# A tuned single-core decoder layer: one block product of the input projection made by seven sub-products, for two pairs of column tiles at once

## The chip, the cores and the metric

The kernel runs on one core of one Trainium2 chip. The metric is the device time of one execution in microseconds (us); the time before is the median of three runs. The engines are named as in the profile: PE (matmul, with PEld for its weight loads), DVE, ACT, POOL, and SP, which here only issues DMAs.

## The reference, cut to what matters

One layer works on 1024 prompt tokens and 8 samples of 8 tokens. Everything starts from one wide projection; the rest (pooling branch, state-space branch, gated merge, output product, final norm) is not touched by the change.

```python
def layer(x, c, pos0, pool_buf, conv_buf, ssm_state, w_ada, b_ada, norm_g, w_in, ...):
    ...
    h = rmsnorm(x, norm_g) * (1 + scale[:, None]) + shift[:, None]
    proj = h @ w_in
    u_pool, z_pool, z_ssm, xbc, dt_raw, g_raw = jnp.split(proj, SPLITS, axis=-1)
    ...
    xbc_c, conv_new = causal_conv(xbc, conv_buf, conv_w, conv_b)
    ...
    x = x + gate[:, None] * (m @ w_o)
```

`h` has 1088 rows (tokens, prompt and samples together) and 1024 columns; `w_in` has 1024 rows and some 8000 columns. Everything is fp32.

## The kernel before, in words

**Numbers in two parts.** PE multiplies fp32r operands. To keep fp32 accuracy each operand is split into a high part (ACT copies it with rounding into a tile `whi`) and a low part (raw minus high, into `wlo`), and each product is three matmuls: high by high, high by low, low by high. `split` (L141) does this for a weight tile: one ACT instruction on L145, one subtraction on L148. In the stages of this case that subtraction is on POOL, the default of its argument `eng`. The parts of `h` stay in SBUF for the whole projection, in `hh_` and `hl_`.

**The projection in pairs.** `w_in` is worked through in pairs of column tiles of 128 columns. For a pair, the product of `h` (two halves of tokens by two halves of the inner dimension: A11, A12, A21, A22) with the weights (two halves of the inner dimension by two column tiles: B11, B12, B21, B22) is made by seven block products instead of eight, in `strassen` (L412). The sums of token blocks (`S1`, `S2`, `S3`, S4 in place of A21) are made once, ahead. The sums of weight blocks (t3 = B22-B12, t2 = t3+B11, t4 = t2-B21, d12 = B12-B11) are made for each pair in `steps` of `pair_w` on L347: three differences of 128x512 on DVE, one on POOL. One block product is one call of `product` (L402): two PSUM banks of 272 tokens, each with 12 matmuls (4 inner tiles by 3 terms), so 24 matmuls; seven of them are 168 matmuls for a pair. Each bank is read when its twelve are done: by ACT on L432 (the first product), by DVE on L419 (sums of partial results `s1`, `u2`, `u3`) or L424 (results of the pair). A12 B21 is one of the seven, and it enters only one of the four results.

**Stages.** 30 pairs go through `product`. The first 20 (the stage between 91 and 520 us, here called the weave) are `heavy` ones, which convolve on DVE (L1088, three instructions of 128x1112 for each column tile) or pool, mixed with `light` ones, which only pass a gate function on ACT and go to DRAM. The last 10 are light ones (`LAST = 10`, 520 to 767 us); between their products the samples' state-space work is put in. In the weave a scheduler sets the order on each engine by priorities and a timeline of its own; in most of the last ten PE's order is that in which the code is written (`in_line`). A pair's weights are prepared while the pair before runs: `between` takes a step of `prep_q` after some products. Beside the weave, `splits` prepares the weights of the two later output products (POOL on L285), one step after each product, paced by `n * 17 // 5`.

**Buffers.** PSUM has eight banks, of tags `mm` (3), `ps` (4) and `pc` (1); in the weave `product` takes them in turn by `banks_`, in the last ten from `ps` and `mm`. There are four `whi` and four `wlo` tiles, three `raw` tiles (sums of weight blocks) and three `rawA` (a column tile as loaded, 512 KB, issued by SP).

Of the kernel before, what the change touches and what calls it, by code (L numbers as in the profile page):

```python
# [8 lines left out]
F32 = mybir.dt.float32  # L9
# [5 lines left out]
PRI = 0  # L15
# [5 lines left out]
P = 128  # L21
# [25 lines left out]
def tile_pool_ssd_step(  # L47
# [89 lines left out]
    scT = const([P, KT, 32], "scT")  # L137
# [4 lines left out]
    def split(raw, kept=None, ncols=P, eng=None):  # L142
        hi = wp.tile([P, 4, P], F32R, tag="whi", name=nm("whi"), bufs=4)
        lo = wp.tile([P, 4, P], F32R, tag="wlo", name=nm("wlo"), bufs=4)
        ins = act(hi[:, :, :ncols], raw[:, :, :ncols], AF.Copy)  # L145
        if kept is not None:
            kept.append(ins.ins)
        (eng or nc.gpsimd).tensor_tensor(lo[:, :, :ncols], raw[:, :, :ncols], hi[:, :, :ncols].bitcast(F32), ALU.subtract)  # L148
# [29 lines left out]
    md = const([P, 16, 9], "md")  # L178
# [82 lines left out]
    def splits():  # L261
# [68 lines left out]
    def pair_w(c0, c1, pri, second, apart=False):  # L330
        def run():
            with tc.high_priority(pri):
                cols = []
# [5 lines left out]
            w = []  # L339

            def add(x):
                with tc.high_priority(pri):
                    w.append(split(x, highs))
# [5 lines left out]
            def steps():  # L349
                t3, t2 = raw_(), raw_()  # L350
                diff(t3, b22, b12)
                yield
                diff(t2, t3, b11, ALU.add)
                if second:

                    t4 = raw_()
                    add(b21)
                    add(t2)
                    add(t3)
                    diff(t4, t2, b21, eng=nc.gpsimd)  # L360
                    yield
                    diff(b12, b12, b11)
                    add(b12)
                    add(t4)
                    add(b22)
                    yield
                    return
                add(t2)
                add(t3)
                yield  # L370
                diff(b12, b12, b11)
                add(b12)
                add(b21)
                diff(t2, t2, b21, eng=nc.gpsimd)
                add(t2)
                add(b22)
                yield
            def apart_():
                t3, t2 = raw_(), raw_()
                fine["n1"] = lambda: add(b21)  # L380
                fine["nt3"] = lambda: diff(t3, b22, b12)
                fine["nt2"] = lambda: diff(t2, t3, b11, ALU.add)
                fine["n2"] = lambda: add(t2)
                fine["nd"] = lambda: diff(b12, b12, b11)

                def rest():
                    t4 = raw_()
                    add(t3)
                    diff(t4, t2, b21, eng=nc.gpsimd)
                    add(b12)  # L390
                    add(t4)
                    add(b22)
# [1896 lines left out]
```

## Time and profile before

| what | value |
|---|---|
| median of 3 runs | 1221.16 us (1219.87 to 1222.5) |
| span of the profiled execution | 1219.3 us |
| PE busy, share of the span | 1203.2 us, 99% |
| PEld busy | 1127.1 us, 92% |
| DVE busy | 937.9 us, 77% |
| POOL busy | 758.1 us, 62% |
| ACT busy | 654.7 us, 54% |
| granted TensorE clock, mean | 0.998 |

The profile gives the profiled execution by its span, from the first to the last instruction: 1219.3 us. The run's own time holds what lies around the span too; against the three times shown that is 0.6 to 3.2 us. Busy shares are means over stages with different limits, so the stages are read apart in what follows. A record of a DVE, ACT or POOL instruction begins when the engine takes it up, and so includes time in which it stands at a port.

### The profile page before, as it was taken

What the parts mean: (1) busy time and instruction counts of PE and PEld (TensorE: products, weight loads), DVE (VectorE), ACT (ScalarE), POOL (GpSimd) and SP (SyncE); (2) the same over time, 40 slices, a digit from 0 to 9 for tenths busy, and PEclk for the clock granted to TensorE, in tenths of its full rate; (3) what the DMA queues carried; (4) which work ended last, traced back from release to release, by engine and by line L of the source; (5) the groups of instructions that cost most, each with busy time, mean ns of one, the idle gap of its engine ahead of it and who ended that gap; (6) DMA issues with size and microseconds to landing.
All of it is one profiled execution on the core that took longest, in us unless ns stands there. A gap on an engine that the chain in (4) does not pass through costs nothing.

```text
span 1219.3 us, 25493 instructions
## 1 busy us (share of the span) xinstructions
PE 1203.2 (99%) x9330; PEld 1127.1 (92%) x9330; DVE 937.9 (77%) x1587; ACT 654.7 (54%) x1491; POOL 758.1 (62%) x677
## 2 busy tenths in 40 slices
PE   9999999999999999999999999999999999999997
PEld 8879999999999999999989899989888898999885
DVE  6993788877989578876676664686877889679976
ACT  6854366565656656454544344566676656312435
POOL 1137868875978778664676766155677758422661
PEclk9999999999999999999999999999999999999999
DMA  9835455564565545443656566898779888585794
GB/s 347 307 136 212 134 155 179 157 232 151 165 188 181 171 149 187 137 143 122 205 187 210 172 198 215 317 314 265 264 257 293 270 279 279 186 313 174 233 213 150
DMA packets 169845, 257.48 MB, mean 211 GB/s; under 512 B 32048, under 2 KB 88120, under 8 KB 169720
## 3 DMA queue, kind: packets, MB, share of 16 engines
q1 hardware_dynamic: 89256, 163.38, 40.3%
q10 hardware_dynamic: 78160, 88.27, 21.4%
q0 software_dynamic: 2304, 4.20, 2.0%
q8 instruction: 74, 1.21, 0.4%
q14 instruction: 51, 0.42, 0.1%
HBM read 170.69 MB, written 85.10 MB: 210 GB/s over the span
## 4 chain that ended last, share of the span: by engine, by line
PE 84%; DVE 6%; DMA 5%; ACT 3%; issue 1%; POOL 1%; SPq 0%; ACTq 0%; DVEq 0%
PE mm L410 23%; PE ps L410 23%; PE mm L221 14%; PE pc L410 5%; PE ps L1256 2%; PE pc L1542 2%; PE ps L2042 2%; PE ps L2040 2%; PE ps L2041 2%; PE ps L1259 2%; DMA wo<-ph 1%; DMA Y<-in_x_prompt 1%; DMA v<-ys 1%; DMA dec<-acs_d 1%; PE ps L1517 1%
## 5 line engine op out<-in xcount | busy, mean ns | idle before, releaser
L148 POOL TENSOR_TENSOR wlo<-rawA,whi 128x512 fp32r<-128x512 f32 x120 | 173.7, 1452 | 81.4 <-ACT whi L145 77.4
L221 PE MATMUL mm<-Y,whi 128*128 128x352 f32 (+1 forms) x960 | 195.7, 334 | 0.8 <-DVE G L1975 0.6
L148 POOL TENSOR_TENSOR wlo<-raw,whi 128x512 fp32r<-128x512 f32 x90 | 149.1, 1665 | 61.4 <-ACT whi L145 51.3
L221 PEld LDWEIGHTS mm<-Y,whi 128*128 128x128 f32 x960 | 159.1, 188 | 7.6 <-issue 4.6
L1088 DVE SCALAR_TENSOR_TENSOR GA<-GA,cvT,GA 128x1112 f32<-128x1112 f32 x72 | 133.8, 1863 | 0.1
L410 PE MATMUL mm<-Y,whi 128*128 128x272 f32 x800 | 119.0, 291 | 0.1
L410 PE MATMUL ps<-Y,whi 128*128 128x272 f32 x800 | 117.4, 289 | 0.0
L145 ACT ACTIVATE whi<-rawA 128x512 fp32r<-128x512 f32 x120 | 75.1, 627 | 76.1 <-PE ps L410 37.7
L145 ACT ACTIVATE whi<-raw 128x512 fp32r<-128x512 f32 x90 | 56.0, 629 | 98.9 <-DVE raw L347 35.2
L410 PEld LDWEIGHTS mm<-Y,whi 128*128 128x128 f32 x800 | 106.8, 188 | 1.8 <-DVE h L1360 0.3
L410 PEld LDWEIGHTS ps<-Y,whi 128*128 128x128 f32 x800 | 106.9, 188 | 0.8 <-issue 0.7
L221 PE MATMUL mm<-Y,wlo 128*128 128x352 f32 (+1 forms) x480 | 98.5, 327 | 0.0
L1244 ACT ACTIVATE dec<-dec,acT 128x128 f32<-128x128 f32 x256 | 78.8, 389 | 29.2 <-POOL dec L1240 29.2
L221 PEld LDWEIGHTS mm<-Y,wlo 128*128 128x128 f32 x480 | 81.7, 188 | 0.0
L1474 POOL TENSOR_TENSOR Y<-xb,Y 128x512 fp32r<-128x512 f32 x32 | 41.2, 1287 | 54.4 <-ACT Y L1472 54.4
L285 POOL TENSOR_TENSOR pw<-pw,ph 128x512 fp32r<-128x512 f32 x40 | 65.8, 1644 | 14.1 <-ACT ph L283 8.2
L410 PE MATMUL mm<-G,whi 128*128 128x272 f32 x480 | 71.4, 290 | 0.0
L410 PE MATMUL ps<-G,whi 128*128 128x272 f32 x480 | 70.4, 289 | 0.0
L410 PE MATMUL ps<-Y,wlo 128*128 128x272 f32 x400 | 66.6, 288 | 0.0
L410 PE MATMUL mm<-Y,wlo 128*128 128x272 f32 x400 | 66.6, 288 | 0.0
L410 PEld LDWEIGHTS mm<-G,whi 128*128 128x128 f32 x480 | 64.0, 188 | 0.9 <-issue 0.4
L410 PEld LDWEIGHTS ps<-G,whi 128*128 128x128 f32 x480 | 64.2, 188 | 0.4 <-issue 0.3
(582 smaller groups left out, 3172.9 us busy)
## 6 DMA issues: line engine op xcount, KB each, us to landing
rawA<-in_w_in SPq DMA_DIRECT2D x62, 512.0 KB
dec<-acs_d SPq DMA_DIRECT2D x32, 512.0 KB
xbc<-GA ACTq DMA_DIRECT2D x24, 512.0 KB
Y<-wo SPq DMA_DIRECT2D x10, 1024.0 KB
pw<-in_w_ssm_out ACTq DMA_DIRECT2D x32, 256.0 KB
ws<-ph ACTq DMA_DIRECT2D x32, 256.0 KB
ws<-pw ACTq DMA_DIRECT2D x32, 256.0 KB
h<-in_state_ssm SPq DMA_DIRECT2D x32, 256.0 KB
```

What stands on the lines that cost most here:

```text
L145: ins = act(hi[:, :, :ncols], raw[:, :, :ncols], AF.Copy)
L148: (eng or nc.gpsimd).tensor_tensor(lo[:, :, :ncols], raw[:, :, :ncols], hi[:, :, :ncols].bitcast(F32), ALU.subtract)
L221: mm(ps[:, :n], w[k // 4][h][:, k % 4, :], r[k][:, o:o + n], start=(j == 0), stop=(j == len(terms) - 1))
L285: nc.gpsimd.tensor_tensor(raw.bitcast(F32R), raw, hi.bitcast(F32), ALU.subtract)
L410: mm(p, w[j // 8][:, k], A(k, s)[j // 4 == 1], start=(j == 0), stop=(j == 11))
L1088: V.scalar_tensor_tensor(d[:, :n], rp[:, k:k + n], cvT[:, 24 * k + mc:24 * k + mc + 1], d[:, :n], ALU.mult, ALU.add)
L1244: act(dec[:, h], dec[:, h], AF.Exp, bias=acT[:, c, 8 * g + h:8 * g + h + 1], scale=-1.0)
L1256: mm(o[hh], xd[:S, 2 * q + hh, :], dec[:S, 2 * q + hh], start=True, stop=state is None)
L1259: mm(o[hh], state[:, h * 64:h * 64 + 64], cE[:, h], start=False, stop=True)
L1474: nc.gpsimd.tensor_tensor(yl[g][:, :, o:o + S], v, yhc.bitcast(F32), ALU.subtract)
L1542: mm(pu, bt, xw.rearrange("p h d -> p (h d)"), start=True, stop=True)
L2040: mm(ps, hi, y[:, k, c0:c0 + cw], start=(first and k == 0), stop=False)
```

## The change

The block product A12 B21 is no longer made for each pair alone. For two pairs in a row (kind "a" and kind "b") the two left column tiles are taken together: A12 (544 tokens by 512) times B21 of both tiles (512 by 256) is again split in 2 by 2 and made by seven sub-products of 272 tokens, 256 inner rows and 128 columns, in a new function `burst`. A sub-product is six matmuls of the same shape as before (2 inner tiles by 3 terms), so the two pairs take 42 matmuls for it where they took 48. 28 of the 30 pairs become 14 such pairs of pairs: nine in the weave, five in the last ten. The sums of A12's blocks (`js1`, `js2`, `js3`, and one that takes the place of A12's own corner) are made once by `joint_operands`, beside the first weave units. The weight sums of the burst are made for each pair of pairs in `joint_steps`, with the subtractions of the low parts on DVE (`eng=V`); the rows of `w_in` that it needs are loaded a second time. A kind-"a" pair begins the preparation of its own six weights in its burst.

Two sums are left in PSUM. In the burst, and in a pair of kind None, A12 B21 is added onto the bank that holds A11 B11, once ACT has read that; and in the weave ("chained") the last product is added onto the banks of the fifth, once DVE has read these, so that DVE's two additions for it go. The rest: two constants move to a pool that is closed earlier, the descriptor scratch of the DMAs that POOL issues goes from 16 KB to 2 KB (these three make room), the pace of `splits` is 19/5, the last ten have 80 steps where they had 70.

```diff
-    scT = const([P, KT, 32], "scT")
+    scT = tfp.tile([P, KT, 32], F32, tag="scT", name="scT", bufs=1)
...
-                at.setdefault(n * 17 // 5 + step, []).append((f, n))
+                at.setdefault(n * 19 // 5 + step, []).append((f, n))
...
+                if meta["kind"] == "a":
+                    for c in (c0, meta["mate"]):
+                        r = raw_()
+                        load(r, tiles_of(c)[:, 4:8])
+                        joint.append(r)
...
+                if meta["kind"] is None:
+                    add("b21", b21)
...
+            def part(x, *names):
+                with tc.high_priority(pri):
+                    hi, lo = split(x, highs, n=2 * len(names), eng=V)
...
+            def joint_steps():
+                wa, wb = joint
+                tt = raw_()
+                diff(tt[:, 2:4], wb[:, 2:4], wb[:, 0:2])
+                diff(tt[:, 0:2], tt[:, 2:4], wa[:, 0:2], ALU.add)
+                yield
+                part(wa, "b11", "b21")
+                diff(wb[:, 0:2], wb[:, 0:2], wa[:, 0:2])
+                part(tt, "t2", "t3")
+                diff(wa[:, 2:4], tt[:, 0:2], wa[:, 2:4])
+                yield
+                part(wb, "d12", "b22")
+                part(wa[:, 2:4], "t4")
+                yield
...
+    def burst(w, ra, rb):
+        def sub(n, x, use, on=None):
+            p = bank_() if on is None else on
...
+            for j in range(6):
+                k = j % 2
+                mm(p, w[n][j // 4][:, k], A(k)[j // 2 == 1], start=(j == 0 and on is None), stop=(j == 5),
+                   skip_group_check=on is not None)
...
+        b1 = sub("b11", "a11", keep)
+        sub("t2", "s2", add(rb[:, 0], ra[:, 0]))
+        yield
+        sub("b21", "a12", keep, on=b1)
+        sub("t3", "s3", add(ra[:, 1], rb[:, 0]))
+        yield
+        b4 = sub("d12", "s1", add(rb[:, 1], ra[:, 1]))
+        sub("t4", "a22", add(ra[:, 1], ra[:, 1], ALU.subtract))
+        yield
+        sub("b22", "s4", add(rb[:, 0], rb[:, 0]), on=b4)
...
+        def fifth(s, p):
+            out(d1, HF, u3, s1)(s, p)
+            if not chained:
+                add(u2, u2)(s, p)
...
+        product(w["b22"], s4_part, out(d1, 0, u2, u2), on=p5 if chained else None)
...
+            if kind == "a":
+                own = steps()
+                next(own)
+                ra, rb = tmp("c2"), tmp("rb")
+                r_next.append(rb)
+                for n, _ in enumerate(burst(jw, ra, rb)):
+                    between("j")
+                    if n == 1:
+                        next(own)
+                    yield
+                next(own)
...
-        if due[0] == 7 * LAST - 4:
+        if due[0] == 8 * LAST - 4:
...
-    nc = _bacc.Bacc("TRN2", target_bir_lowering=False, num_devices=1)
+    nc = _bacc.Bacc("TRN2", target_bir_lowering=False, num_devices=1, dynamic_dma_scratch_size=2048)
```

How the order moves is shown at two places in the weave; `xN` is a row of N equal instructions, and the numbers in the names are those of buffers. First PE, before: the first half of an A12 B21 of one pair (`G` tiles are parts of A12, `whi_558` and `wlo_559` the weights B21, `ps_592` the bank).

```order
L410 MATMUL ps_592_3799<-G_98_760,whi_558_3634 128x272
L410 MATMUL ps_592_3799<-G_100_765,whi_558_3634 128x272
L410 MATMUL ps_592_3799<-G_109_860,whi_558_3634 128x272
L410 MATMUL ps_592_3799<-G_105_846,whi_558_3634 128x272
L410 MATMUL ps_592_3799<-G_99_761,whi_558_3634 128x272
L410 MATMUL ps_592_3799<-G_101_766,whi_558_3634 128x272
L410 MATMUL ps_592_3799<-G_110_861,whi_558_3634 128x272
L410 MATMUL ps_592_3799<-G_106_847,whi_558_3634 128x272
L410 MATMUL ps_592_3799<-G_98_760,wlo_559_3635 128x272
L410 MATMUL ps_592_3799<-G_100_765,wlo_559_3635 128x272
L410 MATMUL ps_592_3799<-G_109_860,wlo_559_3635 128x272
L410 MATMUL ps_592_3799<-G_105_846,wlo_559_3635 128x272
```

The twelve matmuls of a bank stand together, and the high and low weights are used one right after the other. PE after the change, within a burst of the weave (`js1` to `js3` are the sums of A12's blocks; `ps_905` holds the burst's first sub-product, whose own rows stand just ahead and end with the first row here):

```order
L496 MATMUL ps_905_5644<-G_100_765,wlo_884_5531 128x272
L496 MATMUL mm_906_5652<-js2_1429,whi_885_5535 128x272 x4
L496 MATMUL mm_906_5652<-js2_1429,wlo_886_5536 128x272 x2
L496 MATMUL ps_908_5669<-js3_1430,whi_885_5535 128x272 x4
L496 MATMUL ps_908_5669<-js3_1430,wlo_886_5536 128x272 x2
L496 MATMUL mm_915_5696<-G_109_860,whi_891_5577 128x272
L496 MATMUL mm_915_5696<-G_105_846,whi_891_5577 128x272
L496 MATMUL mm_915_5696<-G_110_861,whi_891_5577 128x272
L496 MATMUL mm_915_5696<-G_106_847,whi_891_5577 128x272
L496 MATMUL pc_914_5688<-js1_1428,whi_889_5573 128x272 x4
L496 MATMUL pc_914_5688<-js1_1428,wlo_890_5574 128x272 x2
L496 MATMUL ps_905_5644<-G_109_860,whi_883_5530 128x272
```

Banks now change after six matmuls. The second sum in `ps_905` (last row) has moved behind four other sub-products, and the high half of t4 (`whi_891`) stands apart from its low half, which comes later.

Second DVE, before: in the weave, around the same A12 B21 (L424 and L419 read its banks and those of the next products, L347 makes the next pair's weight sums, L1088 convolves).

```order
L347 TENSOR_TENSOR rawA_533_3445<-rawA_533_3445,rawA_532_3443 128x512
L424 TENSOR_TENSOR u2_539_3456<-u2_539_3456,pc_574_3702 128x272
L424 TENSOR_TENSOR u2_539_3456<-u2_539_3456,mm_575_3717 128x272
L1088 SCALAR_TENSOR_TENSOR GA_531_3441<-GA_482_3147,cvT_134,GA_531_3441 128x1112
L424 TENSOR_TENSOR GA_583_3752<-s1_585_3758,ps_592_3799 128x272
L424 TENSOR_TENSOR GA_583_3752<-s1_585_3758,mm_593_3813 128x272
L419 TENSOR_TENSOR u2_586_3759<-s1_585_3758,ps_595_3829 128x272
L419 TENSOR_TENSOR u2_586_3759<-s1_585_3758,pc_596_3843 128x272
L419 TENSOR_TENSOR u3_587_3760<-u2_586_3759,mm_597_3857 128x272
L419 TENSOR_TENSOR u3_587_3760<-u2_586_3759,ps_598_3871 128x272
L347 TENSOR_TENSOR raw_599_3885<-rawA_578_3742 128x512
```

Mostly bank reads, with one or two SBUF differences among them. DVE after the change, at the end of a kind-"b" pair, where the next burst's weights are prepared (L353 is the line of the differences now, L525 that of the results, L1223 the convolution):

```order
L353 TENSOR_TENSOR raw_648_4139<-raw_648_4139,raw_647_4137 128x256
L148 TENSOR_TENSOR wlo_671_4297<-raw_647_4137,whi_670_4296 128x512
L148 TENSOR_TENSOR wlo_673_4302<-raw_665_4249,whi_672_4301 128x512
L525 TENSOR_TENSOR GA_653_4149<-u3_657_4157,mm_674_4306 128x272
L525 TENSOR_TENSOR GA_653_4149<-u3_657_4157,ps_675_4320 128x208
L353 TENSOR_TENSOR raw_647_4137<-raw_665_4249,raw_647_4137 128x256
L525 TENSOR_TENSOR GA_653_4149<-u3_657_4157,ps_675_4320 128x8x8
L1223 SCALAR_TENSOR_TENSOR GA_646_4135<-GA_611_3901,cvT_134,GA_646_4135 128x1112
L148 TENSOR_TENSOR wlo_677_4337<-raw_648_4139,whi_676_4336 128x512
L525 TENSOR_TENSOR GA_654_4152<-u2_656_4156,ps_667_4260 128x272
L353 TENSOR_TENSOR raw_692_4403<-rawA_650_4143 128x512
L525 TENSOR_TENSOR GA_654_4152<-u2_656_4156,pc_668_4274 128x272
```

Six subtractions and differences with both inputs in SBUF now stand among the bank reads, the L148 rows each behind the ACT instruction that writes its `whi`.

More of the change, by code (lines that the diff above doesn't have):

```diff
@@ L401, in tile_pool_ssd_step, with bank_, product @@
     turn, banks_ = [0], [(PB, PA)]
[L403 removed]
+    def bank_():
+        turn[0] += 1
+        return banks_[0][turn[0] % len(banks_[0])]()[:, :SB]
+    def product(w, A, use, on=None):
+        ps = []
         for s in range(2):
[L405 to L406 removed]
+            p = on[s] if on else bank_()
             for j in range(12):
                 k = j % 4
[L410 removed]
+                mm(p, w[j // 8][:, k], A(k, s)[j // 4 == 1], start=(j == 0 and not on), stop=(j == 11),
+                   skip_group_check=bool(on))
```

232 lines of the change are left out of this document (150 added, 82 removed).

## Prediction

> **What bounds the kernel now.** I read the page first, then the waits of PE, then the projection line by line, then its two stages by windows.
>
> ```profile
> PE 1203.2 (99%) x9330; PEld 1127.1 (92%) x9330; DVE 937.9 (77%) x1587; ACT 654.7 (54%) x1491; POOL 758.1 (62%) x677
> PE 84%; DVE 6%; DMA 5%; ACT 3%; issue 1%; POOL 1%; SPq 0%; ACTq 0%; DVEq 0%
> ```
>
> PE is busy all the time and is 84% of the chain that ended last. A busy PE could still be a waiting one, so the next fence has the line of the projection's matmuls, first what it waited for, then its timeline in the weave (start, duration, what).
>
> ```profile
> its engine sat idle before it (us, times) until:
>   issue: 1.8, 9
>   DVE h L1360: 0.3, 1
> 400.41 1.17 PE L410 MATMUL mm<-Y,whi 128*128 128x272 f32 x8
> 401.42 0.66 PE L410 MATMUL mm<-Y,wlo 128*128 128x272 f32 x4
> 401.92 1.16 PE L410 MATMUL ps<-Y,whi 128*128 128x272 f32 x8
> ```
>
> Over 5040 matmuls PE sat idle for 2.1 us. One bank of twelve begins 1.51 us after the one before it, so a matmul costs 0.126 us there. Now the stages (us, then busy us and count for PE, PEld, DVE, ACT, POOL):
>
> ```profile
> 90.80:519.60 428.80, 428.80 (x3386) 426.05 (x3385) 338.96 (x495) 245.52 (x560) 336.68 (x220) 1.00 0.53 172
> 157.00:240.00 83.00, 83.00 (x664) 83.00 (x663) 74.84 (x105) 48.18 (x112) 66.47 (x42) 1.00 0.55 173
> 240.00:330.00 90.00, 90.00 (x711) 89.31 (x710) 71.25 (x100) 56.04 (x134) 70.63 (x45) 1.00 0.56 182
> 519.60:766.60 247.00, 246.66 (x2004) 232.12 (x2003) 158.54 (x341) 111.61 (x229) 155.27 (x153) 1.00 0.55 184
> ```
>
> PE is the bound in both stages. But in the weave (first row) DVE is at 79%, and in its first loaded stretch (second row) at 90%, while PE loses nothing. The second row gives 83.00/664 = 0.125 us for a matmul; I take that.
>
> **PE's term.** A burst saves 48-42 = 6 matmuls; 14 bursts save 84, nine of them in the weave (54), five in the last ten (30). Same shape, same weight-load size: 84 x 0.125 = 10.5 us less, 6.75 in the weave and 3.75 behind it. Weight loads fall by the same 84. Since PE is on the path throughout, this counts in full wherever nothing else becomes late.
>
> **What it costs DVE.** Prices (min/median/max ns by line, then groups with mean ns of one):
>
> ```profile
> L347 DVE TENSOR_TENSOR raw<-rawA x30: 677/1253/1758, 86.2 to 736.3; 128x512 f32<-128x512 f32 x30
> L148 POOL TENSOR_TENSOR wlo<-raw,whi x90: 1263/1588/2431, 92.2 to 751.8; 128x512 fp32r<-128x512 f32 x90
> L347 DVE TENSOR_TENSOR raw<-rawA 128x512 f32<-128x512 f32 x30 | 33.9, 1131 | 4.2 <-DMA rawA<-in_w_in 4.2
> L642 DVE TENSOR_TENSOR G<-tf,G 128x256 fp32r<-128x256 f32 x4 | 2.7, 665 | 0.0
> L419 DVE TENSOR_TENSOR u<-u,ps 128x272 f32<-128x272 f32 x60 | 25.9, 431 | 13.6 <-PE ps L410 13.6
> L148 POOL TENSOR_TENSOR wlo<-rawA,whi 128x512 fp32r<-128x512 f32 x120 | 173.7, 1452 | 81.4 <-ACT whi L145 77.4
> ```
>
> For each burst DVE gets four differences and one low part of 128x256 and three low parts of 128x512: 5 x 0.665 + 3 x 1.131 = 6.7 us, and five bank reads, 5 x 0.43 = 2.2. In the weave, chaining takes two reads from each of 20 pairs (40 x 0.43 = 17.2), and the two pairs of kind None lose two more each (1.7). The sums of A12's blocks are 24 instructions of 128x272 with two SBUF inputs, once; not in the trace, between 0.43 and 0.665 each; I take 0.55, 13 us. Weave: 9 x 8.9 + 13 - 17.2 - 1.7 = 74 us more, so 339 + 74 = 413 us of 422: 98%. Last ten: 5 x 8.9 = 45, so 204 of 243: 84%.
>
> The price of the subtractions decides this, and it is no constant:
>
> ```profile
> 301.47 0.68 DVE L347 TENSOR_TENSOR raw<-raw,rawA 128x512 f32<-128x512 f32 x1
> 303.26 4.09 POOL L148 TENSOR_TENSOR wlo<-raw,whi 128x512 fp32r<-128x512 f32 x2
> 304.40 1.79 DVE L347 TENSOR_TENSOR rawA<-rawA,rawA 128x512 f32<-128x512 f32 x1
> 306.11 0.42 DVE L424 TENSOR_TENSOR GA<-u,pc 128x272 f32<-128x272 f32 x1
> ```
>
> With POOL idle the difference takes 0.68 us; while POOL subtracts, it takes 1.79, and POOL's own two take 4.09 instead of 2.6. A bank read (one input in PSUM) takes 0.42 beside the same POOL. So a DVE instruction with two SBUF inputs and a POOL instruction run one after the other. All 8 new instructions of a burst are of that kind. Bounds per burst: nobody in the way, 5 x 0.42 (the bank read's price, for half the width) + 3 x 0.68 = 4.1 us; always in the way, 5 x (0.42 + 1.1) + 3 x 1.79 = 13.0, where 1.1 is 1.79-0.68. Weave: 389 to 469 us of 422. I take the means, 413, since POOL also loses two low parts a burst (28 x 1.452 = 41 us in all).
>
> Where does it come late? DVE's 90 us of idle time in the weave is mostly this:
>
> ```profile
> DVE u L419 <- PE ps L410: 24.4, 27, 4.2
> DVE GA L424 <- PE ps L410: 17.3, 23, 2.4
> ```
>
> It waits for PE's next bank, so it is ahead; that idle time goes first at no cost. The 61 us apart from the A12 sums are 0.143 us for each us of weave, which lands on the windows as follows: 157 to 240, 74.84 + 12 = 87 of 81.7, over by 5; 240 to 330, 71.25 + 13 = 84 of 88.6, under. The seven banks in turn, 1.5 us each, let PE run on for some 10 us less what is held. So part of the 5 is absorbed; I charge 3 us to the weave. Its ends are 0 (389 fits in 422) and 47 (469 does not, by 47).
>
> **Weights just in time.** A kind-"a" pair's own six weights now start in its burst, 42 x 0.125 = 5.3 us ahead, where a whole pair was ahead before, and its four joint tiles take all four `whi`. From a freed tile: ACT, then POOL.
>
> ```profile
> L145 ACT ACTIVATE whi<-raw 128x512 fp32r<-128x512 f32 x90 | 56.0, 629 | 98.9 <-DVE raw L347 35.2 <-PE mm L410 17.9 <-PE ps L410 12.4
> L432 ACT ACTIVATE s<-ps x30: 368/379/397, 94.0 to 748.7; 128x272 f32<-128x272 f32 x30
> POOL wlo L148 <- ACT whi L145: 128.7, 81, 5.3
> ```
>
> The t2/t3 tile is free after three sub-products, 2.3 us into the burst; 0.63 + 1.59 = 2.2 gives both parts at 4.5, and the first product of the pair wants them at 5.3 (high) and 7.3 (low, after 16 high matmuls of two banks). It fits, with POOL at its maximum of 2.43 too. The next six at 1.6 each are done faster than products of 3.0 us use them. POOL waits for ACT now, so it has room: price 0 to 1 us a burst, I take 0.1, 1 us in all.
>
> **Sums left in PSUM.** Adding onto a bank needs its first reader to be done. In the weave the order has put 3 us of other matmuls between; in the last ten the second d12 sum follows after one sub-product of t4, 0.75 us, and DVE's read takes 0.43 once it is reached. Slack 0.3 us: with DVE at 84%, one two-input instruction ahead (1.13) overdraws it by 0.8. Between 0 and 1.5 us for each of five bursts; I take 0.2, 1 us. ACT's read for the first bank is 0.38, and sample work stands in that gap.
>
> **At nothing.** 28 loads of 256 KB again on SP: DMA share 0.53 in the weave (first window), cover for 7 MB in 640 us; if the cover went, a burst would wait for them. ACT gets half a high part for each low part that POOL loses and four table loads, 1.28 us each, at 57% busy. Pace and step counts move POOL's work for later stages within a stage in which it waits 129 us. The scratch: POOL issues 16 transfers of its own kind, at the end,
>
> ```profile
> q0 software_dynamic: 2304, 4.20, 2.0%
> R<-in_x_prompt POOLq DMA_DIRECT2D x6, 256.0 KB, 7.5
> ```
>
> 144 packets each, nine for each of 16 DMA engines, landing after some 7.5 us. They come at intervals, so few are under way at once: 0, or up to 7.5 us each for the last few if they had to take turns. The Trainium skill ("DMA: Bandwidth & Descriptors", Anatomy of one DMA and its terms) gives 16 bytes for a descriptor; by it 2 KB hold 128, an estimate of 14 such transfers; no run here shows the ring's size.
>
> **Sum.** -10.5 + 3 + 1 + 1 = -5.5 us. The profiled span is 1219.3 and would be 1213.8; the median of the runs, 1221.16, lies 1.9 above it, so 1215.7.
>
> **Rivals.** (1) Nothing is lost: POOL's 41 us less work shortens DVE's waits, the subtractions come at 0.68 and DVE keeps ahead. For it: PE lost nothing at 90% DVE. Against it: 98%. -10.5: 1210.7.
>
> (2) DVE becomes the bound of the weave, and the kernel is slower. The place is the weave's DVE queue, the mechanism the taking of turns with POOL; each low part on DVE also stands behind ACT's high part and stops the bank reads behind it. For it: 413 of 422 with no idle time at all. If a quarter of today's 90 us of idle stays, DVE needs 413 + 22 = 435, and the weave is 6.7 us longer than its 428.8 now; less 3.75 behind it, +3: 1224. At the always-in-the-way price and no idle time 469, far worse: +36. It decides from about 16 us of idle time that stays. Against it: DVE's idle time is waiting for PE, and the lateness of a bank read costs nothing up to several us. The Trainium skill ("SBUF — State Buffer", Who interferes with whom) states this rule: a DVE instruction with two SBUF inputs and a POOL one that reads SBUF block each other whole. The trace agrees (0.68 against 1.79).
>
> (3) Gain and loss cancel: weights or banks come late by 0.7 us in each burst, 14 x 0.7 = 10: 1221. For it: order after the change puts high and low halves apart, so the parts come close to their use. Against it: the slack worked out above.
>
> **How the numbers follow.** Forecast (-8.5 to -2.5) 0.37; (1) 0.26; (2) 0.22; (3) 0.15. A measurement of this kernel can tell about 0.2%, 2.4 us, from no change. Faster: forecast and (1), 0.63; same: (3) with an edge, 0.14; slower: (2) and the rest of (3), 0.23. The range runs from 1209.5, a little under (1), to 1228, past (2) at its nearer price; beyond lies the far end of (2), and little below. The likeliest case's own range is 1212.7 to 1218.7.
>
> **What would show it.** In the profile after: 84 fewer matmuls; PE busy near 1193; the weave near 425 us and the last ten near 244; DVE in the weave at 94 to 98% with waits for PE's banks nearly gone; subtractions of 128x512 on DVE near 1.1 us. Rival (2) would show PE idle for DVE in the weave, (3) for ACT or POOL at the bursts' lines. The forecast is wrong if the weave is over 430 us.

## The result, and the profile after

The change makes the kernel slower: 1265.21 us (1262.07 to 1275.04) for 1221.68, a ratio of 1.0374 with a 95% interval of 1.0333 to 1.0415. The profiled execution spans 1261.3 us, 42.0 more than before. From its page, the busy times of the engines and the share of the chain that ended last:

```profile
PE 1206.6 (96%) x9246; PEld 1122.0 (89%) x9246; DVE 1002.8 (80%) x1749; ACT 685.1 (54%) x1561; POOL 724.2 (57%) x649
PE 67%; DVE 9%; issue 4%; DMA 3%; POOL 3%; ACT 2%; SPq 0%; ACTq 0%; DVEq 0%; POOLq 0%
```

PE has 84 matmuls fewer, as the change says, and yet 55 us without work where it had 16. It is 67% of the chain, for 84%. The same stages as before by windows (us, then busy us and count of PE, PEld, DVE, ACT, POOL, the granted clock, DMA share, GB/s), the weave first, then the last ten pairs:

```profile
90.30:543.60 453.30, 431.45 (x3332) 423.29 (x3331) 380.86 (x595) 261.62 (x606) 314.00 (x200) 0.99 0.55 173
543.60:802.50 258.90, 245.59 (x1971) 228.62 (x1970) 185.00 (x404) 123.26 (x250) 145.69 (x145) 1.00 0.55 183
```

The weave takes 24.5 us more (453.3 for 428.8), the last ten 12.2 more (258.9 for 246.7), the stretch behind them 5.7 more (458.7 for 453.0). In the weave PE stood idle for 21.9 us, where it had not stood at all, and its waits there were for all three other engines (us, times, longest; the eight largest):

```profile
PE mm L435 <- POOL wlo L148: 5.4, 4, 2.7
PE ps L435 <- POOL wlo L148: 4.0, 5, 1.6
PE pc L435 <- DVE GA L525: 2.5, 1, 2.5
PE mm L435 <- DVE c L503: 2.4, 1, 2.4
PE mm L435 <- DVE s L525: 2.4, 1, 2.4
PE ps L707 <- POOL GA L699: 1.3, 1, 1.3
PE mm L435 <- ACT whi L145: 1.1, 2, 0.6
PE mm L435 <- ACT c L506: 1.1, 1, 1.1
```

From the first burst on nearly all of these fall between 5 and 17 us after the start of a burst. One burst of the weave shows how. Its timeline (start, duration, engine, what, and in brackets the idle time ahead with its releaser), PE first, then DVE, then POOL:

```profile
450.64 0.66 PE L496 MATMUL mm<-js,whi 128*128 128x272 f32 x4
451.14 0.41 PE L496 MATMUL mm<-js,wlo 128*128 128x272 f32 x2
456.57 1.27 PE L435 MATMUL mm<-Y,whi 128*128 128x272 f32 x8 [1.10 <-ACT c L506]
458.63 0.77 PE L435 MATMUL mm<-Y,wlo 128*128 128x272 f32 x4 [0.78 <-POOL wlo L148]
461.83 1.50 PE L435 MATMUL mm<-Y,whi 128*128 128x272 f32 x5 [2.43 <-DVE c L503]
...
450.81 2.16 DVE L1223 SCALAR_TENSOR_TENSOR GA<-GA,cvT,GA 128x1112 f32<-128x1112 f32 x1
452.89 1.50 DVE L148 TENSOR_TENSOR wlo<-raw,whi 128x256 fp32r<-128x256 f32 x1
454.32 0.68 DVE L353 TENSOR_TENSOR raw<-raw,rawA 128x512 f32<-128x512 f32 x1
454.92 0.42 DVE L503 TENSOR_TENSOR rb<-c,ps 128x272 f32<-128x272 f32 x1
455.27 2.18 DVE L689 TENSOR_TENSOR GA<-GA 128x1038 f32<-128x1038 f32 x1
457.37 1.76 DVE L353 TENSOR_TENSOR rawA<-rawA,rawA 128x512 f32<-128x512 f32 x1
459.05 2.38 DVE L1223 SCALAR_TENSOR_TENSOR GA<-GA,cvT,GA 128x1112 f32<-128x1112 f32 x1
461.35 0.42 DVE L503 TENSOR_TENSOR c<-rb,mm 128x272 f32<-128x272 f32 x1
...
450.49 1.30 POOL L285 TENSOR_TENSOR pw<-pw,ph 128x512 fp32r<-128x512 f32 x1
452.11 2.01 POOL L148 TENSOR_TENSOR wlo<-rawA,whi 128x512 fp32r<-128x512 f32 x1 [0.32 <-ACT whi L145]
455.07 1.27 POOL L353 TENSOR_TENSOR raw<-raw,rawA 128x512 f32<-128x512 f32 x1 [0.96 <-DVE raw L353]
456.30 3.95 POOL L148 TENSOR_TENSOR wlo<-raw,whi 128x512 fp32r<-128x512 f32 x2
```

The sub-product t3 (first two rows) is done at 451.55. DVE adds its bank (`c<-rb,mm`) at 461.35, 9.8 us later. The last 6 us of that are a pooling step, a difference and a convolution of about 2 us each, all beside work on POOL: the difference at 457.37 takes 1.76 us, the one at 454.32, with POOL idle, 0.68. PE then stands for 2.43 us for want of that bank. Over all bursts of the weave DVE reads a sub-product's bank on average 5.6 us after its last matmul (45 reads; one in ten comes after more than 10 us). Before the change that was 0.9 us (all 308 of DVE's reads of products' banks in the weave; 0.8 for those of A12 B21).

### The profile page after: what moved, and what is told of

Its sections match the earlier page's. It is cut to its first block, busy times and chain, and to the rows that moved or that the text cites. A ratio compares the mean times of both kernels' runs of the same rounds, so it can differ in the third digit from the quotient of the medians.

```text
span 1261.3 us, 25580 instructions
## 1 busy us (share of the span) xinstructions
PE 1206.6 (96%) x9246; PEld 1122.0 (89%) x9246; DVE 1002.8 (80%) x1749; ACT 685.1 (54%) x1561; POOL 724.2 (57%) x649
## 4 chain that ended last, share of the span: by engine, by line
PE 67%; DVE 9%; issue 4%; DMA 3%; POOL 3%; ACT 2%; SPq 0%; ACTq 0%; DVEq 0%; POOLq 0%
PE mm L221 18%; PE ps L435 13%; PE mm L435 13%; PE ps L1391 3%; PE pc L435 2%; PE pc L1677 2%; PE ps L1394 2%; POOL wlo L148 2%; PE ps L496 2%; PE ps L2190 2%; PE ps L2189 2%; PE ps L2188 2%; PE mm L496 1%; DVE GA L1223 1%; PE ps L1652 1%
## 5 line engine op out<-in xcount | busy, mean ns | idle before, releaser
L148 POOL TENSOR_TENSOR wlo<-rawA,whi 128x512 fp32r<-128x512 f32 x92 | 147.5, 1605 | 95.8 <-ACT whi L145 70.1
L221 PEld LDWEIGHTS mm<-Y,whi 128*128 128x128 f32 x960 | 160.3, 189 | 13.5 <-DVE R L1873 5.9
L148 POOL TENSOR_TENSOR wlo<-raw,whi 128x512 fp32r<-128x512 f32 x90 | 140.3, 1569 | 21.8 <-ACT whi L145 21.0
L145 ACT ACTIVATE whi<-raw 128x512 fp32r<-128x512 f32 (+1 forms) x146 | 87.0, 605 | 95.5 <-PE ps L435 29.9
L435 PE MATMUL ps<-Y,whi 128*128 128x272 f32 x880 | 130.2, 290 | 2.5 <-DVE xd L1422 2.5
L1223 DVE SCALAR_TENSOR_TENSOR GA<-GA,cvT,GA 128x1112 f32<-128x1112 f32 x72 | 128.5, 1789 | 1.3 <-ACT GA L1220 1.3
L435 PEld LDWEIGHTS mm<-Y,whi 128*128 128x128 f32 x864 | 116.0, 189 | 10.7 <-issue 3.7
L435 PEld LDWEIGHTS ps<-Y,whi 128*128 128x128 f32 x880 | 117.6, 188 | 4.2 <-issue 2.9
L145 ACT ACTIVATE whi<-rawA 128x512 fp32r<-128x512 f32 x92 | 57.8, 628 | 69.5 <-PE mm L435 25.2
L221 PEld LDWEIGHTS mm<-Y,wlo 128*128 128x128 f32 x480 | 82.2, 189 | 0.0
L353 POOL TENSOR_TENSOR raw<-raw,rawA 128x512 f32<-128x512 f32 x30 | 44.4, 1481 | 57.7 <-DVE wlo L148 31.9
L435 PEld LDWEIGHTS mm<-Y,wlo 128*128 128x128 f32 x432 | 61.2, 189 | 7.3 <-POOL wlo L148 7.3
L435 PEld LDWEIGHTS ps<-Y,wlo 128*128 128x128 f32 x440 | 61.9, 188 | 3.3 <-POOL wlo L148 3.3
L1670 DVE TENSOR_TENSOR dec<-dec,ps 128x1024 f32<-128x1024 f32 x32 | 38.9, 1216 | 27.6 <-ACT ps L1659 10.4
```

Of the source, the lines that this page charges most:

```text
L145: ins = act(hi[:, :n], raw, AF.Copy)
L148: (eng or nc.gpsimd).tensor_tensor(lo[:, :n], raw, hi[:, :n].bitcast(F32), ALU.subtract)
L221: mm(ps[:, :n], w[k // 4][h][:, k % 4, :], r[k][:, o:o + n], start=(j == 0), stop=(j == len(terms) - 1))
L353: eng.tensor_tensor(dst, x, y, op)
L435: mm(p, w[j // 8][:, k], A(k, s)[j // 4 == 1], start=(j == 0 and not on), stop=(j == 11), skip_group_check=bool(on))
L1223: V.scalar_tensor_tensor(d[:, :n], rp[:, k:k + n], cvT[:, 24 * k + mc:24 * k + mc + 1], d[:, :n], ALU.mult, ALU.add)
```

## The experiments

Stage lengths below are taken from the starts of the first and last matmuls of the projection in the profiled execution; ratios are to the kernel before on the same chip.

| kernel | median us | ratio (95%) | weave | last ten | behind | PE idle, weave / last ten |
|---|---|---|---|---|---|---|
| before | 1221.68 | | 428.8 | 246.7 | 453.0 | 0.0 / 0.3 |
| changed | 1265.21 | 1.0374 (1.0333-1.0415) | 453.3 | 258.9 | 458.7 | 21.9 / 13.3 |
| no_burst | 1244.48 | 1.0189 (1.0174-1.0204) | 428.9 | 267.6 | 457.1 | 0.0 / 14.0 |
| nb17 | 1240.17 | 1.0151 (1.0116-1.0186) | 429.0 | 261.9 | 456.5 | 0.0 / 10.3 |
| nb17_fifth | 1227.87 | 1.0054 (1.0039-1.0069) | 429.0 | 249.1 | 457.6 | 0.0 / 2.0 |
| chain_only | 1222.33 | 1.0000 (0.9990-1.0009) | 429.0 | 249.6 | 451.2 | 0.0 / 2.5 |
| last10 | 1249.91 | 1.0234 (1.0216-1.0251) | 431.7 | 266.7 | 458.0 | 2.3 / 14.7 |
| before_scr | 1228.23 | 1.0061 (1.0038-1.0083) | 428.8 | 246.7 | 462.0 | 0.0 / 0.3 |
| before_scr8 | 1222.66 | 1.0011 (1.0002-1.0020) | 428.8 | 247.3 | 454.2 | 0.0 / 0.8 |
| conv_thin | 1237.52 | 1.0126 (1.0104-1.0148) | 427.9 | 258.1 | 460.4 | 4.4 / 10.6 |
| conv_mid | 1254.22 | 1.0274 (1.0254-1.0294) | 438.2 | 264.5 | 458.7 | 9.7 / 13.2 |
| joint_copy | 1265.26 | 1.0364 (1.0342-1.0387) | 445.0 | 264.9 | 460.9 | 16.2 / 14.5 |
| conv_half | 1287.75 | 1.0546 (1.0519-1.0573) | 472.5 | 268.6 | 458.0 | 31.9 / 14.9 |
| j_nostep | 1265.67 | 1.0362 (1.0341-1.0382) | 447.4 | 268.5 | 460.3 | 16.0 / 14.9 |
| two_yield | 1261.55 | 1.0324 (1.0300-1.0349) | 450.3 | 257.7 | 461.2 | 18.6 / 9.7 |
| no_yield | 1264.36 | 1.0364 (1.0337-1.0392) | 450.7 | 259.9 | 459.5 | 18.4 / 9.7 |
| whi5 | 1269.46 | 1.0387 (1.0347-1.0428) | 455.4 | 260.8 | 460.2 | 20.6 / 11.1 |
| fresh | 1281.53 | 1.0489 (1.0473-1.0504) | 457.9 | 269.0 | 460.5 | 25.4 / 15.9 |
| pool_low | 1282.92 | 1.0506 (1.0487-1.0526) | 461.2 | 270.5 | 457.8 | 26.1 / 14.4 |
| free_pe | 1330.41 | 1.0892 (1.0857-1.0926) | 520.2 | 265.5 | 459.5 | 70.2 / 16.8 |

### What is not the bursts: the order in the last ten, and the scratch

no_burst takes the pairing out (`a["kind"], b["kind"] = "a", "b"` is gone, no `joint_operands`, 70 steps):

> The changed kernel without bursts: every pair makes A12 B21 for itself again (onto the bank of A11 B11), all else stays (2 KB scratch, the 19/5 pace, both sums in PSUM, the constants). The program's matmuls are those of before. Theory 'weights' (a burst uses up weight tiles twice as fast, its parts hold all four, and the pair's own parts are made too late behind it) and theory 'DVE' (the eight added subtractions of a burst make DVE late with the banks): both 1218 to 1225, no loss is left. Theory 'the rest' (scratch, pace or the sums in PSUM cost the 44 us): 1250 or more.

It gave 1244.48, between the two expectations: the weave is as before, so its 24.5 us are the bursts' own. But 23 us stay, 20.9 of them in the last ten. last10 keeps the bursts in the last ten alone (`paired = [... for u in light[-LAST:]]`):

> Bursts in the last ten pairs only; the 20 pairs of the weave make A12 B21 for themselves. If each stage's loss is its own (weights or DVE, both): the weave takes 427 to 431 us as before, the last ten 257 to 261 as in the changed kernel (before: 247), the sum some 1232 to 1240. If the last ten are late only because of what the weave hands on: last ten 243 to 248 and a total near 1217 to 1222.

The weave falls back to 431.7, but the last ten take 266.7, no less than without bursts: neither expectation. nb17 is no_burst with `n * 17 // 5`, since its weave has fewer steps to pace by:

> The kernel without bursts of the first experiment, with the old pace of the later stages' weight preparation (17/5, not 19/5). Without bursts the weave has fewer steps, and at 19/5 some jobs were left for the start of the last ten, where PE stood for 2.4 us. If that pace costs the 21 us of the last ten: 1220 to 1225, last ten 247 to 250. If only that start: last ten 261 to 265, total 1237 to 1241. If the order of A12 B21 in a pair (third, on the bank of the first product) costs the rest: unchanged beyond that start.

That is 4.3 us in the medians and 5.7 in the last ten, as expected for their start alone (last10 has this part too). nb17_fifth goes back to the order of before in the last ten, in strassen:

```diff
-        if r is None:
+        if r is None and not late:
             product(w["b21"], a_part(0, 1), second_, on=p1)
+        if late:                                   # behind d12
+            product(w["b21"], a_part(0, 1), out(d0, 0, s1, c2))
```

> As the kernel beside it (no bursts, pace 17/5), and in the last ten A12 B21 is made as before the change: fifth in the pair, in banks of its own, added by DVE. Theory 'held banks' (the first product's two banks are kept through three products in the fixed order of the last ten, and ACT's read of them comes late): last ten 247 to 251, total 1220 to 1227. If that order isn't the cause (but the first weights, now made a step later): last ten 258 or more, total 1232 or more.

In this kernel the addition reads a buffer that the fifth product has already overwritten, so of it only the time counts. The last ten by windows, nb17 first and then nb17_fifth:

```profile
519.90:781.80 261.90, 251.57 (x2001) 236.44 (x2001) 152.03 (x320) 112.20 (x231) 151.93 (x152) 0.98 0.52 174
```

```profile
520.40:769.50 249.10, 247.05 (x2002) 232.08 (x2000) 162.95 (x340) 114.31 (x231) 153.13 (x152) 1.00 0.55 182
```

And PE's longest waits there in nb17 (us, times, longest):

```profile
PE mm L435 <- DVE h L1495: 5.9, 5, 2.2
PE ps L1429 <- ACT c L538: 2.4, 1, 2.4
```

With A12 B21 on the banks of A11 B11, two banks are kept through three products, and PE waits for banks that the samples' work (L1495) and ACT's reading (L538) still hold; with banks of its own and its old place in the pair 12.8 us go. (Place and banks changed together; which of them counts isn't told apart.) This cost is one of pairs without bursts in the fixed order, and doesn't stand in the changed kernel, whose last ten have bursts.

Of the 6.8 us that are left in nb17_fifth, 4.6 lie behind the projection. before_scr is the kernel before with `dynamic_dma_scratch_size=2048`, before_scr8 with 8192:

> The kernel before with the descriptor scratch of 2 KB and nothing else changed. After the last ten pairs every kernel with the change's other parts took 4 to 7 us longer than before (456 to 460 us for 453), bursts or not. If the scratch is the cause: 1224 to 1229. If not (my zero for it holds): 1219 to 1223.

> The kernel before with a descriptor scratch of 8 KB. At 2 KB the stretch behind the projection was 9 us longer (DMAs of SP that were issued later). If the cost grows evenly as the scratch shrinks: 1223 to 1226. If there is a size below which transfers begin to wait, and 8 KB lies above it: 1219 to 1223.

Both hold the same instructions in the same order on every engine as before. At 2 KB the weave and the last ten are untouched to 0.1 us, and the stretch behind takes 9.0 us more in the profile, 7.6 in the medians; at 8 KB it is about 1 us. PE's waits there at 2 KB (us, times, longest), and two windows at the change of stage:

```profile
PE mm L221 <- DVE R L1725: 3.2, 1, 3.2
PE ps L1519 <- DMA xb<-xbc: 2.8, 1, 2.8
```

```profile
769.00:776.00 7.00, 4.04 (x25) 3.75 (x24) 1.52 (x3) 3.64 (x10) 0.00 (x0) 0.96 1.06 395
776.00:783.00 7.00, 6.71 (x26) 6.62 (x27) 3.47 (x6) 6.75 (x20) 2.14 (x2) 0.56 0.31 120
```

PE waits for loads of the next stage at a moment when the DMA engines are full (share 1.06), and the clock, 1.00 in that second window before, is 0.56 behind the wait. Why loads that SP issues land later with a smaller scratch for POOL's is not seen: SP's issues behind the projection take 146.6 us for 143.0, no more than at 8 KB (146.9). In the changed kernel the first of these waits is 5.6 us (L1873 is that line there) and the stretch behind 5.7 longer; that this is the scratch's there too was not tried. chain_only takes all three costs out (no bursts, the order of before in the last ten with the buffer mended, 16 KB, pace 17/5) and keeps the sums of the weave in PSUM:

> What is left of the change without bursts, without the small scratch (16 KB again), with the pace of before, and in the last ten with A12 B21 fifth in the pair in banks of its own, as before; the sums in PSUM of the weave stay. If the three costs found are all there are: weave 429, last ten 247 to 249, 452 to 454 behind, total 1219 to 1224. If another part costs something: above 1225.

1222.33 us, a ratio of 1.0000: nothing else in the change outside the bursts costs anything, and the 40 bank reads that chaining saves bring nothing.

### The weave: what DVE has to do

conv_thin cuts the convolution to `d[:, :64]`, conv_mid to `d[:, :740]`; conv_half makes two instructions of 556 columns of each; joint_copy turns the joint differences and low parts into `V.tensor_copy`:

> The changed kernel with the convolution's 72 DVE instructions cut from 1112 to 64 columns; most of the convolution is left out, its waits stay. DVE has some 115 us less to do in the weave. Theory 'DVE': the weave falls from 453 to 423-430 us and the waits of PE for DVE and ACT bank reads go; total 1232 to 1240. Theory 'weights': PE still waits for POOL's low parts behind the bursts (some 10 us in the weave), weave 433 to 445, total 1242 to 1254.

> The changed kernel with the convolution's DVE instructions cut to 740 of 1112 columns (the rest of the convolution is left out). DVE then has some 338 us to do in the weave, as before the change (339). Theory 'sum' (DVE's load decides): weave 427 to 434, total 1235 to 1243. Theory 'bunching' (in a burst banks are used up twice as fast and long instructions stand in front of their reads, whatever the sum): weave 437 to 446, total 1245 to 1255.

> The changed kernel with each convolution instruction made as two of 556 columns: the same work, some 5 us more for the 72 more instructions, but a bank read waits behind pieces of 0.7 to 1.3 us instead of 1.4 to 2.4. Theory 'bunching': weave 436 to 447, total 1244 to 1256. Theory 'sum': weave 453 to 460, total 1262 to 1270.

> The changed kernel with the eight added DVE instructions of a burst turned into copies of the same tiles with one input each; the sums and low parts of the burst's weights are left out, counts and waits stay, the pair's own parts too. Theory 'turns' (the added instructions with two SBUF inputs take turns with POOL and make DVE late): weave 426 to 438 for 453, total 1235 to 1248. Theory 'banks' (a burst uses up a bank in 0.75 us instead of 1.5, so that seven banks cover half the lateness that they covered before, whatever DVE does): weave 445 to 453, total 1254 to 1263.

Their weaves by windows, one row each in this order (DVE is the third busy time):

```profile
90.30:518.20 427.90, 423.48 (x3332) 419.45 (x3331) 297.55 (x598) 265.66 (x609) 257.57 (x200) 1.00 0.58 185
```

```profile
90.80:529.00 438.20, 428.46 (x3332) 422.45 (x3331) 348.92 (x597) 263.58 (x608) 294.37 (x200) 0.99 0.57 180
```

```profile
91.20:563.70 472.50, 440.56 (x3333) 430.96 (x3332) 405.34 (x661) 261.27 (x604) 284.51 (x200) 0.97 0.52 166
```

```profile
90.00:535.00 445.00, 428.83 (x3332) 421.71 (x3331) 361.95 (x594) 262.27 (x604) 306.27 (x200) 1.00 0.56 176
```

In these runs the weave follows DVE's work: 298, 349, 362, 381 (the changed kernel) and 405 us of DVE make 428, 438, 445, 453 and 473 us of weave. That is the theory of DVE's sum, but not of the sum alone: further below, runs with 368 to 383 us of DVE have weaves of 447 to 461. And with 349 us, 10 more than before the change, conv_mid still loses 9.7 us where before lost none, as the theory of bunching had it: the bursts have made nearly the same load dearer. Whether smaller pieces would help stays open (conv_half: its 72 more instructions cost DVE 24 us, not the 5 that I had expected, and it missed both ranges). joint_copy made most of the added instructions short and free of POOL (last section), and yet the weave fell by 8.3 of its 24.5 us only, to the edge of what "banks" had said; so turns of the added instructions with POOL are hardly the whole of the loss. In conv_thin PE no longer waits for POOL's low parts either, which speaks against the theory of weights by itself. Its bank reads in bursts come 1.3 us late on average for 5.6, and POOL's own instructions are shorter. The low parts of the weave on POOL (count, busy us, mean ns of one, then the idle time ahead), in the changed kernel and then in conv_thin:

```profile
L148 POOL TENSOR_TENSOR wlo<-rawA,whi 128x512 fp32r<-128x512 f32 x60 | 104.3, 1741 | 46.9 <-ACT whi L145 34.8 <-DVE GA L525 4.9 <-DMA pw<-in_w_ssm_out 4.6
```

```profile
L148 POOL TENSOR_TENSOR wlo<-rawA,whi 128x512 fp32r<-128x512 f32 x60 | 82.7, 1379 | 32.3 <-ACT whi L145 31.4 <-PE ps L435 0.6
```

1741 ns fall to 1379 without an edit to them. pool_low (`split(...)` without `eng=V`) moves the joint low parts to POOL:

> The changed kernel with the low parts of the joint weights on POOL, where all other low parts are made, not on DVE. Theory 'DVE': DVE gets 26 us of the weave and 14 us of the last ten back, and at least a third of the 44 us goes: 1250 or less. Theory 'weights': POOL gets 52 more instructions of 0.65 to 2.4 us in the same chain from ACT to PE, and its parts come later still: 1265 to 1290.

It was worse, 1282.92, in the range of the theory of weights: POOL's 48 us more in the weave (361.7) hurt more than DVE's 4 fewer helped (377.3). Whether by later low parts or by longer turns for DVE isn't told apart; PE's waits in the weave for low and high parts rise from 10.5 to 14.1 us.

### The weave: how the bursts are served

whi5 has `bufs=5` for `whi` (the `stc` tiles cut from four to two for room), fresh sends `b21` and `b22` of a burst to banks of their own, j_nostep drops `between("j")`, no_yield drops the steps inside bursts wholly, two_yield has two of them and the old paces:

> The changed kernel with five tiles for high parts of weights instead of four (room from two fewer small tiles). Theory 'weights' (the joint parts hold all four, so that ACT and POOL can't work ahead): PE's waits for POOL's low parts (9.9 us) shrink to under 3 and the time to 1240 to 1252. Theory 'banks' or 'turns': 1255 to 1267, since banks are read late all the same.

> The changed kernel with the two sums of each burst not left in PSUM: both sub-products go to banks of their own and DVE adds them (two more bank reads a burst, 0.43 us each, one ACT read less). Theory 'held banks' (PE waits for the first reader of a bank onto which it adds): PE's waits for ACT's reads in the bursts (4.3 us here, 2.7 of them at once in the last ten) go, total 1254 to 1260. Theory 'DVE': 14 x 0.86 = 12 us more for DVE, total 1261 to 1272.

> The changed kernel without the four steps of other work that it puts into each burst (in the weave these are convolution instructions of 1.3 to 2.4 us on DVE, four in a stretch in which PE makes 5.3 us of matmuls; they now fall to the pair's products). Same instructions, another order. Theory 'bunching' (DVE has room over the weave, 381 of 453 us, but too much falls on the bursts): the weave falls from 453 to 430-443, total 1238 to 1252. Theory 'sum' (DVE with its turns with POOL is full anyway): weave 450 to 458, total 1258 to 1266.

> The changed kernel with bursts that take no steps of other work at all: neither convolutions nor the later stages' weights nor the samples' work is put between sub-products; these are paced by products alone (pace 29/10, 60 steps in the last ten). Theory 'steps' (work handed out by the number of calls is four times as dense in a burst): weave 430 to 442, last ten 245 to 252, total 1228 to 1245. Theory 'banks' or 'weights': weave 444 to 456, last ten 255 or more, total 1253 to 1270.

> The changed kernel with two steps of other work in a burst instead of four: a pair of pairs then has 14 steps, as two pairs had before, and the pace (17/5) and the 70 steps of the last ten are those of before. If the rhythm of the samples' steps is what the last ten lose by: last ten 244 to 250 for 259. If not: 257 to 265. In the weave, where four convolution steps in a burst become two: 445 to 453. Total 1240 to 1252 or 1255 to 1265.

A fifth tile for high parts brings nothing (PE's waits for POOL's low parts even rise to 14.6 us). But `wlo` stayed at four, and the limit moved there. In the changed kernel POOL's low parts in the weave wait for ACT's high parts (44.1 us) and never for a matmul of the projection to be done with one; in whi5 it is the other way round (POOL's waits, us, times, longest):

```profile
POOL wlo L148 <- PE mm L496: 10.6, 2, 9.6
POOL wlo L148 <- PE ps L435: 9.5, 7, 4.3
POOL wlo L148 <- PE pc L496: 9.2, 1, 9.2
```

So this run doesn't clear the tiles; more of both kinds at once is untested. fresh is some 15 us worse, beyond both its ranges: two more reads a burst at DVE, and two banks more used; the sums kept in PSUM save more than their waits cost. Fewer steps in the bursts bring 3 to 6 us of the weave's 24.5: the bunching of these steps is a part, and a small one. None of the rhythms brings the last ten back.

### The last ten

> The changed kernel, with PE's order in the last ten pairs left to the scheduler instead of fixed to that of the code. Theory 'fixed order' (a late bank or sample step stops PE there because nothing else may go ahead): last ten 245 to 253 for 259, total 1248 to 1257. Theory 'load' (DVE and ACT have more to do there and PE's work is late whatever the order): 256 to 270, total 1259 to 1275.

free_pe drops `in_line((mybir.EngineType.PE,), True)`, and that did the opposite of what I meant: the later call then fixes PE's order from further back, and it is the weave that came into the order of the code:

```profile
90.70:610.90 520.20, 449.97 (x3332) 441.48 (x3331) 383.47 (x596) 267.30 (x607) 290.62 (x200) 0.91 0.48 151
```

So it doesn't answer its question, but another: with the same load on DVE (383 us), the weave in fixed order loses 70 us of PE, in the scheduler's 22. Putting other matmuls ahead of late banks is worth 48 us there, and the last ten don't have it.

Which part of the bursts costs the last ten stays open. Held banks (fresh), the two-input form of the added work (joint_copy), tiles (whi5) and the number of steps (two_yield, no_yield) left 9.7 to 15.9 us of idle time each. PE's largest waits there in the changed kernel (us, times, longest):

```profile
PE mm L496 <- ACT c L506: 2.7, 1, 2.7
PE ps L1272 <- DMA s<-dts_d: 2.5, 2, 1.5
PE ps L435 <- DVE xd L1422: 2.5, 2, 1.7
```

The first is ACT's read of a bank that a burst adds onto; the others, with smaller ones 8.0 us of the 13.3, are for the samples' work. DVE's reads of the projection's banks are named for 1.9 us, and in these five bursts they come 0.7 us late on average (25 reads), not 5.6. So the late reads of the weave are not what costs here. The first two pairs of the last ten lose most; their rows, after and before:

```profile
543.60:598.50 54.90, 48.41 (x364) 45.23 (x363) 43.68 (x92) 29.95 (x53) 22.67 (x26) 1.00 0.44 143
```

```profile
519.60:569.00 49.40, 49.40 (x387) 47.85 (x386) 38.23 (x75) 25.16 (x50) 28.02 (x31) 1.00 0.33 115
```

DVE has 5.5 us more to do there and PE stands for 6.5, 4.5 of it for the samples' work; that DVE's greater load makes that work late is argued, not shown.

## Why the prediction was wrong

The forecast was 1215.7 us, a gain of 0.4%; the kernel became 3.7% slower. Its profiled span is 47.5 us over the 1213.8 of the sum: some 27 in the weave, some 15 in the last ten, 6 behind.

**PE's term** was right: 84 matmuls fewer, still 0.125 us each between waits. Without any wait the weave would have been 422.

**DVE's sum** was too high: 381 us in the weave, not 413. Low parts of 128x512 took 0.72 us on average, not 1.13, and the differences and low parts of 128x256 0.60, not 0.67; the sums of A12's blocks 21, not 13. The sum also left the old instructions at their old price: the pairs' own 60 differences of 128x512 fell from 1.20 to 0.99 us (14 us in all) and the convolutions from 1.87 to 1.79. Rival (1) had said that with less work on POOL the subtractions would come at less; in this it was right, and the kernel lost time all the same.

**The step that failed** is the one behind it: "The seven banks in turn, 1.5 us each, let PE run on for some 10 us less what is held." In a burst a bank is used up by six matmuls, 0.75 us. The same seven banks then cover 5.3 us, just where DVE, ACT and POOL have the preparation of the next weights, the convolution steps and denser bank reads. I judged lateness by stretches of 80 to 90 us, where DVE kept within PE's time; the reads come 5.6 us late on average in the bursts. The 3 us charged to the weave were 31.3, the time by which it misses 422: 25 us in the steps between matmuls that have idle time in them (21.9 us of it idle), 3 of half clock and 3 of slowed matmuls. That the shorter cover by the banks is the reason is worked out from these figures; no run gave the bursts more banks.

**Weights just in time** (0.1 us a burst) were mis-sized: PE waited 9.9 us in ten waits for POOL's low parts. The working there took POOL's 1.59 us and tiles freed in time. In the weave of the changed kernel the mean is 1.71, and POOL waits 44.1 us for ACT, which waits 68.8 us there for PE to be done with `whi` tiles. conv_thin, where these waits of PE are gone, shows that they hang on DVE's load too.

**Sums in PSUM** were 1 us in the sum; PE's waits for ACT's reads of them (L506) are 4.3 us, but fresh shows that without them it is worse.

**The scratch** was costed at nothing, and "the ring" was thought to matter for POOL's own 16 transfers alone. It costs 7.6 us by itself in the kernel before; the changed kernel's stretch behind is 5.7 us longer.

**The last ten** were to be 3.75 us shorter, less 1 for held banks, and were 12.2 longer. The step that failed there is the price of 0.2 us a burst for held banks as the only cost, with DVE at 84%. PE's waits are mostly for the samples' work and for one ACT read; which part of the bursts makes these late stays open.

**The clock** had no term at all (below).

Of the rivals, (2) had the side and the place: "DVE becomes the bound of the weave". Its turns with POOL are in the rows, but by joint_copy they are hardly the whole, and DVE was no bound by its sum: the price of 1224 took a quarter of DVE's idle time to stay; in fact 72 us of it stayed (453.3 - 380.9), of the 90 that there were, and it was late all the same. Rival (3) named the weights and banks that come late at the bursts. They were put down as two cases with a price each; conv_thin, in which both go with DVE's load, says that in the weave they are one lateness seen at two queues. The last ten (12 us) I had only in (3), at a third of the price.

## What to carry to other kernels

An engine's share of a stage says little about a piece of work that comes in bursts: count, for the burst alone, how long the buffers last at the burst's rate and how late the reader is there, with the longest instruction of its queue in front of it. Smaller products use banks and weight tiles faster, so work saved on a bound engine is paid in slack on the others. What is changed to make room (a scratch, a pace) is tried by itself on the old kernel first: here that was one run, and 7.6 us.

## What the hardware showed that I had not expected

**Short idle times halve the clock.** Four windows of the changed kernel, each 3.41 us, two and two:

```profile
458.19:461.60 3.41, 0.77 (x4) 0.55 (x4) 3.41 (x3) 0.56 (x2) 3.41 (x4) 1.00 0.38 98
461.60:465.01 3.41, 3.18 (x14) 3.18 (x15) 3.31 (x8) 1.18 (x3) 1.30 (x2) 0.50 0.84 268
601.60:605.01 3.41, 1.68 (x13) 1.68 (x14) 2.41 (x6) 3.02 (x6) 1.28 (x1) 1.00 0.50 151
605.01:608.42 3.41, 3.41 (x28) 3.18 (x27) 2.45 (x7) 3.37 (x11) 1.67 (x2) 1.00 0.60 205
```

With 2.64 us of idle time in a window the next one had half the clock (14 matmuls started for 28), with 1.73 it had not. The changes of clock stand on a fixed grid of 3.41 us. In the 20 profiles, from 70 us on and up to PE's last matmul, all 74 such windows at full clock with 1.9 us or more of idle time were followed by one at half clock, 13 of 28 with 1.6 to 1.9, 1 of 273 with 0.5 to 1.6, and none of 6347 below. So a wait of 2 us can cost 1.7 more (the 14 matmuls that did not start), or by these counts nothing if it lies half in one window and half in the next; this may be why single stages differ by some us between kernels that hardly differ. The Trainium skill ("TensorE: Matmul & The Clock Gate", Part 1: The HAM clock gate) gives a free-running window of 4096 cycles, 3413 ns, and the half clock after an idle window. The trace agrees on the window; it needs to be idle for only some 55% of it.

**Some copies take turns too.** The casts of joint_copy, one input each, ran from 280 to 1527 ns:

```profile
L151 DVE CAST wlo<-whi x56: 280/420/1527, 129.5 to 754.3; 128x512 fp32r<-128x512 f32 x42, 128x256 fp32r<-128x256 f32 x14
```

Of the 14 casts of 128x256, 13 took 0.50 to 1.39 us, each beside a POOL instruction; of the 42 of 128x512, 40 took 0.41 to 0.42. The copies that stand for the differences took 0.28 to 0.30 in 51 of 56 cases. So that run shortened the added instructions (DVE 19 us less in the weave) and took most of them out of POOL's way, but not all. The Trainium skill ("SBUF — State Buffer", Who interferes with whom) says that copies and casts in the two-port modes hold the shared ports; the longest of these rows agree.
